# First two token tiles in large rows over both hardware queues ahead of the weights, half-chunk first weights; last store contiguous, last sum seeded in PSUM

## The chip, the cores and the metric

The kernel runs on all 8 cores of one Trainium2 chip, each core on its own share of the batch with the same weights and no exchange between the cores. The metric is the device time of the slowest core, in microseconds (us).

A run on all eight cores has two states. In the fast state every core shows a mean granted TensorE clock of 0.998 to 1.000. In the slow state the cores of one die, or of both, show less (a mean of 0.81 to 0.99), and the run is 1% to 21% longer. In the slow profile of the kernel before, on its slowest core, the clock is 0.81 in some stretches and 1.00 in others (0.81 from 260 to 270 us, 1.00 from 280 to 360), with TensorE busy in both. Only fast runs, or the cores of an undisturbed die in a slow run, are compared below.

## The reference, cut to what matters

```python
def rmsnorm(x, g):
    y = x * rsqrt(mean(x * x, axis=-1, keepdims=True) + EPS)
    return y * g

def swiglu(h, w_gate, w_up, w_down):
    return (silu(h @ w_gate) * (h @ w_up)) @ w_down

for i in range(4):                                   # layers
    x = x + 0.5 * rmsnorm(swiglu(rmsnorm(x, g[0]), ...first FFN...), g[1])
    x = x +       rmsnorm(mixer(rmsnorm(x, g[2])), g[3])   # gated convolution or causal pooling
    x = x + 0.5 * rmsnorm(swiglu(rmsnorm(x, g[4]), ...second FFN...), g[5])
```

The width is 1,024 features (8 chunks of 128) and the FFN is 2,816 wide (22 chunks). Each core does two passes over 1,056 tokens, held as three tiles of 352 tokens, with the features on the 128 partitions.

## The kernel before

The program is a list of operations that a small scheduler in Python puts into a fixed order on each engine, before anything runs. It knows the engines' durations, and it has a model of DMA: one serial pipe.

```python
# Sched.run(): when the result of an operation is assumed to be visible
            vis = o.end
            if o.dma:
                s0 = max(dma_free, st + (2.8 if e == "pool" else 1.0))
                dma_free = s0 + o.dma[1] / 170e3
                vis = dma_free + 1.5
```

The start of the program, which the change rewrites. Queues: `sp` and `act` are hardware queues, `pool` is the GpSimd queue, which carries all weights in this program; they are converted from f32 to bf16 on the way (the page of the kernel before counts 636.49 MB read from HBM and 339.98 MB in DMA packets):

```python
    # earlier in the program: params on the sp queue, 128 rows of 1 KB
    LEAD = 2

    def first_group(finish, pre):
        load_x(0, 0, ("sp", "act", "sp", "act"), 4, -3)        # tile 0 in quarters, 2,816 B rows
        slots = [load_ab(0, 0, jj) for jj in range(LEAD)]      # weight chunks 0 and 1 (1 MB each)
        load_x(0, 1, "pool", 2)                                # tile 1 behind them
        slots += [load_ab(0, 0, jj) for jj in range(LEAD, GRP)]
        load_wdn(0, 0)
        load_x(0, 2, "pool", 2)
        warm(72, ["ones"])                                     # warm-up matmuls with ones
        prenorm(0, 0, 0, pre=False, parts=(2, 2, 2, 1, 1))     # statistics of tile 0 in five groups
        prenorm(0, 0, 1, pre=False)
        prenorm(0, 0, 2)
        for k in range(GRP + LEAD):
            if k < GRP:
                ffn_ab(0, 0, k, slots[k], k == 0)              # tile 0 leads by two chunks
            if k >= LEAD:
                ffn_ab(1, 1, k - LEAD, slots[k - LEAD])
        # ... cut: down projections, tile 2
```

The statistics of a tile are eight squares on ScalarE, summed over the features by matmuls with a matrix of ones:

```python
    def norm_stats(t, src, key, off, parts=(8,)):
        v = S.vt(stat=True)
        for c in range(NCH):
            S.op("act", lambda a, c=c: a.activation(out=h[t][:, c, :], in_=src[:, c, off:off + TS], func=AF.Square), ...)
        # ... cut: matmuls with ones in groups of `parts`, then Ln and Exp on ScalarE give rr = 1/rms
```

The end: the last tile's down projection in halves of 176 tokens. For each chunk, VectorE adds the PSUM sum to the accumulator, ScalarE squares it; then Ln, Exp, two wide multiplications and additions, and the store:

```python
        for dc, hc in pairs:
            def fo(pe, v=v, dc=dc, c0=c0):
                for jj in range(GRP):
                    mm = pe.matmul(B(v)[:, 0:HW], lhsT=wdn[dc][...], rhs=gt[u][:, jj, c0:c0 + HW],
                                   start=(jj == 0), stop=(jj == GRP - 1))
                return mm
            S.op("dve", ... out=acc, in0=B(v)[:, 0:HW], in1=acc, op=ALU.add ...)
            S.op("act", ... out=sq, in_=acc, func=AF.Square ...)
            # ... cut
            for q in range(2):
                # ... cut: acc *= rr; x += acc, four chunks at a time
                S.op("sp", lambda e, o=o, c0=c0: e.dma_start(
                    out=y_o[p, t].rearrange("p (a b) -> p a b", b=TS)[:, o:o + 4, c0:c0 + HW],   # 704 B rows
                    in_=x[t][:, o:o + 4, c0:c0 + HW]), ...)
```

## Time and profile before

| | us |
|---|---|
| fast runs | 4354.1, 4354.21 |
| slow runs | 4509.77, 5136.39 |
| span of the profiled run (slow, clock 0.974 on its slowest core) | 4453.2 |

The profile of the kernel before fell in the slow state, so its 4,453 us is not a time to compare with. The head and the tail can still be read from it, with that in mind.

From the page of the kernel before: the first line of part 1 (busy us, share of the span, instructions), the ScalarE queue's line of part 3 (packets, MB, share of the DMA engines) and two groups of part 5 (busy us, mean ns of one, idle time before them and what ended it).

```profile
PE 4430.3 (99%) x29109; PEld 2878.7 (65%) x29109; DVE 2187.6 (49%) x3807; ACT 1743.8 (39%) x3053; POOL 460.6 (10%) x973
...
q10 hardware_dynamic: 288, 0.72, 0.1%
...
L357 PE MATMUL ps<-h,ring 128*128 128x352 bf16 x19200 | 2981.6, 318 | 4.9 <-DVE h L357 4.9
...
L357 PE MATMUL ps<-gt,wdn 128*128 128x352 bf16 (+1 forms) x9304 | 1423.8, 315 | 0.6 <-DVE gt L357 0.6
```

TensorE is busy 99% of the span. Nothing that leaves the 28,504 weight matmuls alone can move the time by more than what lies before the first and after the last of them, and the few us of gaps in between. All instructions carry one line number, because one helper emits them; so they are told apart by their tiles: `ring` holds gate and up weights, `wdn` down weights, `x` the tokens, `h` the squares and then the normalised tokens, `rr` 1/rms.

The head, from the timeline of the kernel before on its slowest core (start us, duration us, engine, operation, out<-in, count, idle time before it and what ended it):

```profile
7.17 1.65 ACT L357 ACTIVATE h<-x 128x352 bf16<-128x352 f32 x4 [3.59 <-DMA x<-x_in]
...
11.73 1.65 ACT L357 ACTIVATE h<-x 128x352 bf16<-128x352 f32 x4 [2.91 <-DMA x<-x_in]
...
13.44 1.35 PE L357 MATMUL ps<-h,ones_bf 128*128 128x352 bf16 x4 [3.24 <-ACT h L357]
...
15.39 0.46 ACT L357 ACTIVATE rr<-ps 128x352 f32<-128x352 f32 x1
...
15.89 4.05 DVE L357 SCALAR_TENSOR_TENSOR h<-x,params_sb,rr 128x352 bf16<-128x352 f32 x8
...
16.62 7.73 PE L357 MATMUL ps<-h,ring 128*128 128x352 bf16 x32 [1.83 <-DVE h L357]
...
26.80 1.37 PE L357 MATMUL ps<-h,ones_bf 128*128 128x352 bf16 x8 [2.44 <-ACT h L357]
...
28.00 4.19 PE L357 MATMUL ps<-h,ring 128*128 128x352 bf16 x27
```

The same stretch in the fast profile of this kernel (first experiment), on its slowest core; the count of the last row ends where the query's window ended:

```profile
15.30 0.46 ACT L357 ACTIVATE rr<-ps 128x352 f32<-128x352 f32 x1
...
16.52 6.73 PE L357 MATMUL ps<-h,ring 128*128 128x352 bf16 x32 [1.83 <-DVE h L357]
...
26.90 5.27 PE L357 MATMUL ps<-h,ring 128*128 128x352 bf16 x23
```

Four squares run on an early half of tile 0 at 7.17 and the other four when its second half is there, at 11.73. Statistics, Ln, Exp and the first normalised chunk follow, and the first weight matmul starts at 16.62. TensorE pauses once more at 26.8, for the statistics of tile 1, and from 28.0 it doesn't stop.

The tail, from the chain of waits of the kernel before (start us, duration us, what):

```profile
4429.96 12.47 PE ps L357 x162
...
4444.64 0.26 DVE acc L357
4444.90 0.02 issue
4444.93 0.36 ACT sqf L357
...
4446.40 1.69 DVE acc L357 x2
4448.09 0.80 DVE x L357
```

After the last weight matmul come a sum on VectorE, a square, Ln and Exp, wide VectorE work and the store: some 8.8 us on this core, in which TensorE has only the last statistics to do.

### The profile page before, as it was taken

The numbers are of one execution on the slowest core, as the hardware profiler recorded it, in microseconds if no ns is written. First come the engines' busy times: TensorE is split into PE (matmuls) and PEld (weight loads), VectorE is DVE, ScalarE is ACT, GpSimd is POOL, SyncE is SP. The second block draws the span as 40 slices with busy tenths as digits, with TensorE's granted clock in tenths as the row PEclk, the third lists the DMA queues.
The fourth block names the chain that finished last, engine by engine and source line by source line (L and its number), as shares of the span: only waits on it lengthen the run. The fifth ranks groups of instructions, "written<-read, shape, count | busy, mean of one in ns | idle before, by whom it ended". The sixth has DMA issues, their size and how long they took to land.

```text
span 4453.2 us, 68545 instructions; the slowest of 8 cores (4392.4 to 4453.2 us)
## 1 busy us (share of the span) xinstructions
PE 4430.3 (99%) x29109; PEld 2878.7 (65%) x29109; DVE 2187.6 (49%) x3807; ACT 1743.8 (39%) x3053; POOL 460.6 (10%) x973
## 2 busy tenths in 40 slices
PE   9999999999999999999999999999999999999999
PEld 5666666666666666666666666666666666666666
DVE  2376261755347525175434753527452474352844
ACT  3244242643334424264333442326433344232643
POOL 1021000000002100000000210000000021000000
PEclk9999999999999999999999999999999999999999
DMA  7445444434344544443544354444443334444441
GB/s 134 68 76 90 79 79 79 79 53 73 60 68 70 86 79 79 79 79 67 107 93 71 62 86 79 79 79 79 70 77 60 65 58 80 79 79 79 79 77 43
DMA packets 106673, 339.98 MB, mean 76 GB/s; under 512 B 11904, under 2 KB 15360, under 8 KB 106368
## 3 DMA queue, kind: packets, MB, share of 16 engines
q0 software_dynamic: 98352, 315.40, 43.4%
q1 hardware_dynamic: 7728, 19.48, 1.3%
q8 instruction: 229, 3.75, 0.4%
q10 hardware_dynamic: 288, 0.72, 0.1%
q14 instruction: 76, 0.62, 0.1%
HBM read 636.49 MB, written 11.55 MB: 146 GB/s over the span
## 4 chain that ended last, share of the span: by engine, by line
PE 99%; DVE 0%; DMA 0%; ACT 0%; issue 0%; DVEq 0%; ACTq 0%
PE ps L357 99%; DMA x<-x_in 0%; ACT h L357 0%; DVE acc L357 0%; DVE h L357 0%; DVE x L357 0%; ACT ps L357 0%; ACT rr L357 0%; DVEq L375 0%; DVE gt L357 0%; ACT sa L357 0%; ACT acc L357 0%; ACTq L357 0%; ACT sqf L357 0%
## 5 line engine op out<-in xcount | busy, mean ns | idle before, releaser
L357 PE MATMUL ps<-h,ring 128*128 128x352 bf16 x19200 | 2981.6, 318 | 4.9 <-DVE h L357 4.9
L357 PEld LDWEIGHTS ps<-h,ring 128*128 128x128 bf16 x19200 | 1905.3, 99 | 1042.9 <-DVE h L357 4.7
L357 PE MATMUL ps<-gt,wdn 128*128 128x352 bf16 (+1 forms) x9304 | 1423.8, 315 | 0.6 <-DVE gt L357 0.6
L357 DVE TENSOR_TENSOR gt<-ps,sa 128x352 bf16<-128x352 f32 x1056 | 551.5, 523 | 1668.6 <-PE ps L357 1623.6
L357 PEld LDWEIGHTS ps<-gt,wdn 128*128 128x128 bf16 x9304 | 914.7, 99 | 484.6 <-DVE gt L357 1.0
L357 ACT ACTIVATE sa<-ps 128x352 f32<-128x352 f32 x1152 | 533.8, 464 | 1516.5 <-PE ps L357 1484.4
L357 POOL DMA_DIRECT2D ring<-wab x352 | 186.8, 532 | 2681.4 <-PE ps L357 2672.1
L357 ACT ACTIVATE acc<-ps 128x352 f32<-128x352 f32 x480 | 222.5, 465 | 466.0 <-PE ps L357 466.0
L357 DVE TENSOR_TENSOR h<-h 128x704 f32<-128x704 f32 (+1 forms) x404 | 320.4, 793 | 69.0 <-ACT h L357 66.5
L357 ACT ACTIVATE h<-acc 128x352 bf16<-128x352 f32 (+2 forms) x181 | 145.9, 814 | 473.3 <-DVE acc L357 450.2
L357 DVE TENSOR_TENSOR acc<-ps,acc 128x352 f32<-128x352 f32 (+1 forms) x392 | 202.5, 517 | 255.4 <-PE ps L357 254.4
L357 ACT ACT_TABLE_LOAD x239 | 306.6, 1283 | 7.6 <-PEq L400 2.0
L357 DVE SCALAR_TENSOR_TENSOR h<-x,params_sb,rr 128x352 bf16<-128x352 f32 x480 | 246.7, 578 | 117.6 <-ACT rr L357 117.4
L357 ACT ACTIVATE h<-x 128x704 f32<-128x704 f32 (+2 forms) x266 | 216.0, 832 | 56.6 <-DVE x L357 29.8
L357 DVE TENSOR_TENSOR x<-x,acc 128x1408 f32<-128x1408 f32 (+1 forms) x146 | 232.9, 1596 | 0.2
L357 DVE SCALAR_TENSOR_TENSOR acc<-acc,params_h,rr 128x352 f32<-128x352 f32 x376 | 198.0, 578 | 43.0 <-ACT rr L357 42.9
L357 POOL DMA_DIRECT2D wdn<-wd x256 | 135.6, 534 | 327.8 <-PE ps L357 327.5
L357 DVE SCALAR_TENSOR_TENSOR scr<-scr,params_sb 128x352 f32<-128x352 f32 (+1 forms) x192 | 112.1, 584 | 9.2 <-ACT scr L357 8.7
L357 ACT ACTIVATE scr<-scr,params_sb 128x352 f32<-128x352 f32 (+1 forms) x96 | 56.7, 591 | 95.5 <-DVE scr L357 95.5
L357 ACT ACTIVATE ps<-ps,epst 128x352 f32<-128x352 f32 (+1 forms) x145 | 76.2, 526 | 35.3 <-PE ps L357 31.5
L357 DVE TENSOR_TENSOR scr<-ps,sa 128x352 f32<-128x352 f32 (+2 forms) x128 | 54.8, 428 | 36.1 <-PE ps L357 34.1
L357 POOL COPY scr<-convh 128x2 f32<-128x2 f32 x96 | 42.3, 446 | 266.3 <-DVE pinit L357 177.2
(58 smaller groups left out, 889.4 us busy)
## 6 DMA issues: line engine op xcount, KB each, us to landing
ring<-wab POOLq DMA_DIRECT2D x352, 512.0 KB, 10.9
wdn<-wd POOLq DMA_DIRECT2D x256, 352.0 KB, 14.9
ring<-wci POOLq DMA_DIRECT2D x29, 768.0 KB, 12.1
wdn<-wco POOLq DMA_DIRECT2D x32, 256.0 KB, 11.6
y_o<-x SPq DMA_DIRECT2D x10, 704.0 KB, 3.2
x<-x_in SPq DMA_DIRECT2D x6, 704.0 KB, 6.9
x<-x_in POOLq DMA_DIRECT2D x4, 704.0 KB, 37.0
scr<-spool SPq DMA_DIRECT2D x4, 608.0 KB, 10.8
```

The costliest lines, as they stand in the source:

```text
L357: ins = attr(*a, **k)
```

## The change: its intent and its diff

The intent is a shorter head and a shorter tail. In the head, tiles 0 and 1 go in halves, in rows of 5,632 B, to both hardware queues, ahead of the weights in the program; the first weight chunk comes in two halves, so that TensorE can begin with half of it; four of the eight squares go to VectorE; more warm-up matmuls; and the lead of two chunks is dropped, because both tiles are expected together. In the tail, the last sum is seeded in PSUM by a ScalarE copy, so that the matmuls add to it, and the stores are contiguous and the last is split over two queues.

```diff
+    def norm_stats(t, src, key, off, parts=(8,), dsq=0):
         for c in range(NCH):
+            if c >= NCH - dsq:
+                S.op("dve", lambda v_, c=c: v_.tensor_tensor(out=h[t][:, c, :], in0=src[...], in1=src[...], op=ALU.mult), ...)
+                continue
             S.op("act", ... func=AF.Square ...)
 ... (cut)
     def first_group(finish, pre):
-        load_x(0, 0, ("sp", "act", "sp", "act"), 4, -3)
-        slots = [load_ab(0, 0, jj) for jj in range(LEAD)]
-        load_x(0, 1, "pool", 2)
-        slots += [load_ab(0, 0, jj) for jj in range(LEAD, GRP)]
+        load_x(0, 0, ("sp", "act"), 2, -3)
+        S.op("sp", lambda e: e.dma_start(out=params[:], in_=params_d), 0.06, writes=["params"], dma="params", nbytes=70000, prio=-3)
+        small_params()
+        load_x(0, 1, ("sp", "act"), 2, -3)
+        slots = [[load_units(wab[0, 0][:, i * 1024:(i + 1) * 1024], 1)[0] for i in range(2)]]
+        slots += [load_ab(0, 0, jj) for jj in range(1, GRP)]
         load_wdn(0, 0)
         load_x(0, 2, "pool", 2)
-        warm(72, ["ones"])
-        prenorm(0, 0, 0, pre=False, parts=(2, 2, 2, 1, 1))
-        prenorm(0, 0, 1, pre=False)
+        warm(115, ["ones"])
+        prenorm(0, 0, 0, pre=False, parts=(4, 2, 2), dsq=4)
+        prenorm(0, 0, 1, pre=False, parts=(4, 2, 2), dsq=4)
         prenorm(0, 0, 2)
-        for k in range(GRP + LEAD):
-            if k < GRP:
-                ffn_ab(0, 0, k, slots[k], k == 0)
-            if k >= LEAD:
-                ffn_ab(1, 1, k - LEAD, slots[k - LEAD])
+        for k in range(GRP):
+            ffn_ab(0, 0, k, slots[k], k == 0)
+            ffn_ab(1, 1, k, slots[k], k == 0)
 ... (cut: the convolution history waits for the first weights; tail:)
+            seed = (hc, dc) == (1, NCH - 1)
+            if seed:
+                S.op("act", lambda a, ...: a.activation(out=B(v)[:, 0:HW], in_=acc[t][:, dc, a0:a0 + HW], func=AF.Copy), ...)
-                                   start=(jj == 0), stop=(jj == GRP - 1))
+                                   start=(jj == 0 and not seed), stop=(jj == GRP - 1), skip_group_check=seed)
 ... (cut: with seed, no VectorE sum, and the squares read PSUM)
-                S.op("sp", ... out=y_o[p, t].rearrange("p (a b) -> p a b", b=TS)[:, o:o + 4, c0:c0 + HW] ...)
+                S.op("act" if (hc, d) == (1, 4) else "sp", ...
+                        out=y_o[p, t][:, (hc * NCH + d) * HW:(hc * NCH + d + n) * HW] ...)    # 2,816 or 1,408 B rows
```

That the matmuls add to what ScalarE has written is shown here by results alone: every experiment below with the seed (e2 to e7, e9 to e12) is marked correct in the record. By the program's order an earlier matmul has written the bank; a seed in a bank that none had written was not run.

More of the change, by code (lines that the diff above doesn't have):

```diff
@@ L467, in build_program @@
     P_STAT, P_EV, P_CH = -2, 0, 1
-    S.op("sp", lambda e: e.dma_start(out=params[:], in_=params_d), 0.06, writes=["params"], dma="params", nbytes=90000)
     S.op("dve", lambda v: v.memset(ones_bf[:], 1.0), 0.2, writes=["ones"])
@@ L478, in build_program @@
             S.op("pool", lambda v, g=g, i=i: v.memset(invc[:, g, i:i + 1], 1.0 / (i + 1)), 0.2, writes=[("invc", g)], prio=-2)
-    S.op("dve", lambda v: v.tensor_scalar(out=params_h[:], in0=params[:, 0:192], scalar1=0.5, scalar2=None, op0=ALU.mult),
-         0.3, reads=["params"], writes=["params_h"])
-    S.op("dve", lambda v: v.tensor_copy(out=pscale[:].rearrange("p a b -> p (a b)"), in_=params[:, 240:256]), 0.2,
-         reads=["params"], writes=["pscale"])
-    S.op("dve", lambda v: v.tensor_scalar(out=pscale[:, :, 0:2], in0=pscale[:, :, 0:2], scalar1=0.5, scalar2=None, op0=ALU.mult),
-         0.2, reads=["pscale"], writes=["pscale"])
-    for j in range(2):
-        gp = ((2 * j + 1) * 6 + 3) * 8
-        S.op("dve", lambda v, j=j, gp=gp: v.tensor_tensor(out=pgain[:, j], in0=pscale[:, j], in1=params[:, gp:gp + 8], op=ALU.mult),
-             0.2, reads=["pscale", "params"], writes=[("pgain", j)])
     st = {"ru": 0, "ld": 0, "q": 0, "u": 0, "z": 0, "w": 0}
@@ L521, in stat_finish @@
              2 * c_act(TS) + 0.15, reads=["eps"], writes=[("rr", b)], vts=[v], prio=P_CH, margin=0.2, tbl="lnexp", wvt=True)
-    def norm_stats(t, src, key, off, parts=(8,)):
+    def norm_stats(t, src, key, off, parts=(8,), dsq=0):
         v = S.vt(stat=True)
         for c in range(NCH):
+            if c >= NCH - dsq:
+                S.op("dve", lambda v_, c=c: v_.tensor_tensor(out=h[t][:, c, :], in0=src[:, c, off:off + TS], in1=src[:, c, off:off + TS], op=ALU.mult),
+                     c_dve(TS), reads=[(key, t, c)], writes=[("h", t, c)], prio=P_CH, margin=0.1)
+                continue
             S.op("act", lambda a, c=c: a.activation(out=h[t][:, c, :], in_=src[:, c, off:off + TS], func=AF.Square),
@@ L585, in norm_stats_out, with prenorm @@
         stat_finish(t, v)
-    def prenorm(l, n, t, to_u=False, pre=True, parts=(8,), ag=False):
+    def prenorm(l, n, t, to_u=False, pre=True, parts=(8,), ag=False, dsq=0):
         b = t % 2
@@ L591, in prenorm @@
         else:
-            norm_stats(t, x[t], "x", 0, parts)
+            norm_stats(t, x[t], "x", 0, parts, dsq)
         if ag:
@@ L718, in ffn_out_last, with fo @@
             c0, a0 = hc * HW, PAD + hc * HW
-            def fo(pe, v=v, dc=dc, c0=c0):
+            seed = (hc, dc) == (1, NCH - 1)
+            if seed:
+                S.op("act", lambda a, v=v, dc=dc, a0=a0: a.activation(out=B(v)[:, 0:HW], in_=acc[t][:, dc, a0:a0 + HW], func=AF.Copy),
+                     c_act(HW), reads=[("acc", t, dc), ("out", dc - 3)], vts=[v], prio=P_EV)
+            def fo(pe, v=v, dc=dc, c0=c0, seed=seed):
                 for jj in range(GRP):
                     mm = pe.matmul(B(v)[:, 0:HW], lhsT=wdn[dc][:, jj * 128:(jj + 1) * 128], rhs=gt[u][:, jj, c0:c0 + HW],
-                                   start=(jj == 0), stop=(jj == GRP - 1))
+                                   start=(jj == 0 and not seed), stop=(jj == GRP - 1), skip_group_check=seed)
@@ L724, in fo @@
                 return mm
-            S.op("pe", fo, GRP * 0.081, reads=[("g", u, jj) for jj in range(GRP)] + [("wdn", dc)], vts=[v])
+            S.op("pe", fo, GRP * 0.081, reads=[("g", u, jj) for jj in range(GRP)] + [("wdn", dc)], writes=[("out", dc)], vts=[v])
             ak = ("accl", hc, dc)
-            S.op("dve", lambda v_, v=v, dc=dc, a0=a0: v_.tensor_tensor(
-                out=acc[t][:, dc, a0:a0 + HW], in0=B(v)[:, 0:HW], in1=acc[t][:, dc, a0:a0 + HW], op=ALU.add),
-                c_dve(HW), reads=[("acc", t, dc)], writes=[ak], vts=[v], prio=P_EV)
@@ L730, in ffn_out_last @@
-            S.op("act", lambda a, dc=dc, a0=a0, hc=hc: a.activation(out=sq[hc][:, dc, 0:HW], in_=acc[t][:, dc, a0:a0 + HW], func=AF.Square),
-                 c_act(HW, True), reads=[ak], writes=[("sq", hc, dc)], prio=P_EV)
+            if not seed:
+                S.op("dve", lambda v_, v=v, dc=dc, a0=a0: v_.tensor_tensor(
+                    out=acc[t][:, dc, a0:a0 + HW], in0=B(v)[:, 0:HW], in1=acc[t][:, dc, a0:a0 + HW], op=ALU.add),
+                    c_dve(HW), reads=[("acc", t, dc)], writes=[ak], vts=[v], prio=P_EV)
@@ L732, in ffn_out_last @@
+            y = lambda v=v, dc=dc, a0=a0, seed=seed: B(v)[:, 0:HW] if seed else acc[t][:, dc, a0:a0 + HW]
+            S.op("act", lambda a, dc=dc, hc=hc, y=y: a.activation(out=sq[hc][:, dc, 0:HW], in_=y(), func=AF.Square),
+                 c_act(HW, True), reads=[] if seed else [ak], writes=[("sq", hc, dc)], vts=[v] if seed else [], prio=P_EV)
             g = gcol(l, 5, dc)
-            S.op("act", lambda a, dc=dc, a0=a0, g=g: a.activation(out=acc[t][:, dc, a0:a0 + HW], in_=acc[t][:, dc, a0:a0 + HW], func=AF.Copy,
-                                                                 scale=params_h[:, g:g + 1]),
-                 c_act(HW, True) + 0.09, reads=[ak, "params_h"], writes=[ak], prio=P_CH)
+            S.op("act", lambda a, dc=dc, a0=a0, g=g, y=y: a.activation(out=acc[t][:, dc, a0:a0 + HW], in_=y(), func=AF.Copy,
+                                                                      scale=params_h[:, g:g + 1]),
+                 c_act(HW, True) + 0.09, reads=["params_h"] + ([] if seed else [ak]), writes=[ak], vts=[v] if seed else [], prio=P_CH)
@@ L754, in ffn_out_last @@
             bc = bass.AP(rv.tensor, rv.offset, [list(rv.ap[0]), [0, 4], [1, HW]])
-            for q in range(2):
-                o = 4 * q
+            tb_ = (t + 2 * hc) % NTILE
+            yb = hq[tb_].rearrange("p a b -> p (a b)").rearrange("p (a b) -> p a b", b=HW)
+            yk = [("h", tb_, c) for c in range(NCH)]
+            for o in (0, 4):
                 ks = [("accl", hc, o + i) for i in range(4)]
@@ L760, in ffn_out_last @@
                     c_dve(4 * HW), reads=ks + [("rr", hc)], writes=ks, prio=P_CH)
-                S.op("dve", lambda v_, o=o, a0=a0, c0=c0: v_.tensor_tensor(
-                    out=x[t][:, o:o + 4, c0:c0 + HW], in0=x[t][:, o:o + 4, c0:c0 + HW], in1=acc[t][:, o:o + 4, a0:a0 + HW], op=ALU.add),
-                    c_dve(4 * HW), reads=ks + xk, writes=[("xl", hc, q)], prio=P_CH)
-                S.op("sp", lambda e, o=o, c0=c0: e.dma_start(
-                    out=y_o[p, t].rearrange("p (a b) -> p a b", b=TS)[:, o:o + 4, c0:c0 + HW], in_=x[t][:, o:o + 4, c0:c0 + HW]), 0.06,
-                    reads=[("xl", hc, q)], dma=f"yl{hc}{q}", nbytes=4 * HW * 256, final=True)
+                for d, n in ((o, 4),) if hc == 0 or o == 0 else ((o, 2), (o + 2, 2)):
+                    S.op("dve", lambda v_, d=d, n=n, a0=a0, c0=c0, yb=yb: v_.tensor_tensor(
+                        out=yb[:, d:d + n, :], in0=x[t][:, d:d + n, c0:c0 + HW], in1=acc[t][:, d:d + n, a0:a0 + HW], op=ALU.add),
+                        c_dve(n * HW), reads=ks + xk, writes=[("yl", hc, d)] + yk, prio=P_CH)
+                    S.op("act" if (hc, d) == (1, 4) else "sp", lambda e, d=d, n=n, hc=hc, yb=yb: e.dma_start(
+                        out=y_o[p, t][:, (hc * NCH + d) * HW:(hc * NCH + d + n) * HW],
+                        in_=yb[:, d:d + n, :].rearrange("p a b -> p (a b)")), 0.06,
+                        reads=[("yl", hc, d)], dma=f"yl{hc}{d}", nbytes=n * HW * 256, final=True)
     def load_ab(f, g, jj):
@@ L787, in ffn_group, with small_params @@
                 ffn_out(g, t, u, finish, pre(t))
-    LEAD = 2
-    def first_group(finish, pre):
-        load_x(0, 0, ("sp", "act", "sp", "act"), 4, -3)
-        slots = [load_ab(0, 0, jj) for jj in range(LEAD)]
-        load_x(0, 1, "pool", 2)
-        slots += [load_ab(0, 0, jj) for jj in range(LEAD, GRP)]
+    def small_params():
+        S.op("dve", lambda v: v.tensor_scalar(out=params_h[:], in0=params[:, 0:192], scalar1=0.5, scalar2=None, op0=ALU.mult),
+             0.3, reads=["params"], writes=["params_h"])
+        S.op("dve", lambda v: v.tensor_copy(out=pscale[:].rearrange("p a b -> p (a b)"), in_=params[:, 240:256]), 0.2,
+             reads=["params"], writes=["pscale"])
+        S.op("dve", lambda v: v.tensor_scalar(out=pscale[:, :, 0:2], in0=pscale[:, :, 0:2], scalar1=0.5, scalar2=None, op0=ALU.mult),
+             0.2, reads=["pscale"], writes=["pscale"])
+        for j in range(2):
+            gp = ((2 * j + 1) * 6 + 3) * 8
+            S.op("dve", lambda v, j=j, gp=gp: v.tensor_tensor(out=pgain[:, j], in0=pscale[:, j], in1=params[:, gp:gp + 8], op=ALU.mult),
+                 0.2, reads=["pscale", "params"], writes=[("pgain", j)])
+    def first_group(finish, pre):
+        load_x(0, 0, ("sp", "act"), 2, -3)
[4 more added lines that the diff above has]
+        slots += [load_ab(0, 0, jj) for jj in range(1, GRP)]
         load_wdn(0, 0)
         load_x(0, 2, "pool", 2)
-        warm(72, ["ones"])
-        prenorm(0, 0, 0, pre=False, parts=(2, 2, 2, 1, 1))
-        prenorm(0, 0, 1, pre=False)
+        warm(115, ["ones"])
+        prenorm(0, 0, 0, pre=False, parts=(4, 2, 2), dsq=4)
+        prenorm(0, 0, 1, pre=False, parts=(4, 2, 2), dsq=4)
         prenorm(0, 0, 2)
-        for k in range(GRP + LEAD):
-            if k < GRP:
-                ffn_ab(0, 0, k, slots[k], k == 0)
-            if k >= LEAD:
-                ffn_ab(1, 1, k - LEAD, slots[k - LEAD])
+        for k in range(GRP):
+            ffn_ab(0, 0, k, slots[k], k == 0)
+            ffn_ab(1, 1, k, slots[k], k == 0)
         ffn_out(0, 0, 0, finish, True)
@@ L914, in conv_mixer @@
         S.op("sp", lambda e: e.dma_start(out=chist[:].rearrange("p a b -> p (a b)"), in_=sconv[j, p]), 0.06,
-             writes=["chist"], dma="chist", nbytes=65536)
+             reads=[("ru", 0)], writes=["chist"], dma="chist", nbytes=65536)
         slots = [load_units(wci[j, c], 3) for c in range(NCH)]
@@ L1035, in load_x @@
                                                  in_=x_in[p, t][:, n * i * TS:(i + 1) * n * TS]), 0.55 if eng == "pool" else 0.1,
-                 writes=[("x", t, c) for c in range(n * i, n * i + n)], dma=f"x{eng}{t}{i}", nbytes=n * TS * 350, prio=-1 if eng == "pool" else prio)
+                 writes=[("x", t, c) for c in range(n * i, n * i + n)], dma=f"x{eng}{t}{i}", nbytes=n * TS * (350 if eng == "pool" else 271), prio=-1 if eng == "pool" else prio)
     def store_y(p, t):
@@ L1151, in unpack @@
         pss = np.asarray(r["ps_s"]).reshape(2, NPASS, 128, NCH, NSS, 19)[..., 4:19].transpose(0, 1, 4, 5, 3, 2)
+        yl = np.asarray(r["y_o"])[-1, -1].reshape(128, 2, NCH, TS // 2)
+        y[-1, NTOK - TS:] = yl.transpose(1, 3, 2, 0).reshape(TS, D)
         for p in range(NPASS):
```

## The prediction

> **What bounds the kernel now.** The page has TensorE 99% busy and the chain of waits 99% TensorE: 28,504 weight matmuls (19,200 + 9,304) of 315 to 318 ns. The change touches none of them, only the two ends, which are small (slowest core, 4):
>
> - Head (timeline). Token tile 0 lands at 11.7 us; its first weight matmul starts at 16.6; 32 of them (4.8 us at full rate) are done before 28.0, when TensorE stops pausing. So the head loses 28.0 - 4.8 = 23.2 us: 22 to 23 on cores 1, 3, 4, 7, about 20 on 0, 2, 5, 6, whose tile 0 landed at 9.2 to 9.9 us.
> - The DMA engines are over 90% busy from 4 us on (stretch table)[...]: a contest for bytes.
> - The granted clock is 0.50 in 15-20 us; four statistics matmuls took 1.35 us against 0.77 warm.[...]
> - Tail (chain of waits): last weight matmul to end of span about 8.8 us, of it DVE sum 0.34, square 0.36, Ln and Exp 0.7, wide DVE work 3.3, and over 3 us of store.
>
> **What the change does.**
> 1. Tiles 0 and 1 in 5,632 B rows on both hardware queues; tile 1 no longer behind 2 MB of weights. [...]the DMA table shows one packet per row (288 for two 128-row loads and completions)[...]. Estimate, from 0.72 MB in 4.0 to 4.5 us now: tile 0 at about 10 us (-1.5), tile 1 at 15 to 18 instead of 20 to 22. But all eight squares now follow the landing (about 2.1 us, DVE and ACT sharing, against 1.66), and weights get less.
> 2. [...]last statistics about 0.5 us against 1.37. Landing to first weight matmul: 4.9 to about 4.5.
> 3. The lead of two chunks goes. Each chunk feeds 4.8 us of TensorE[...], but tile 1's normalisation (0.5 us a chunk on DVE against 0.15 a matmul) is now exposed, where tile 0's next chunk covered it. This gives back part: head -2 us (+1 to -5) on the slow cores.
> 4. Tail: the seed in PSUM saves the last DVE sum, -0.4; rows of 1,408 to 2,816 B instead of 704 and a half-sized last store, -0.6.
>
> The body is unchanged but for ripples of list scheduling; its gaps (3.2, 1.1, 1.1 us) stay.
>
> **Predicted:** 4354.2 - 3 = **4351 us**, 80% range **4341 to 4362**[...]. Chances: faster by over 2% 0.01, within 2% 0.97, slower by over 2% 0.02 (only if the slow state takes the median; one of three runs before was 5136).
>
> **What would show it.** Tile 0's squares start near 10 us on cores 1, 3, 4, 7; clock 1.0 when weight matmuls start; head loss about 21 us; last weight matmul to end near 7.8; body equal.
>
> **What would make it wrong.** Tile 1 landing at 20 us, so that TensorE stands before it and the head grows; or at 13, and the head shrinks by 6; first weights starved; a changed body order.

The sum is -2 for the head and -1 for the tail (-0.4 and -0.6), together the -3 in 4354.2 - 3 = 4351. The gain of the tokens from larger rows (tile 0 at about 10 us, tile 1 at 15 to 18) and the last statistics in about 0.5 us stand as estimates. (Of the 288 packets, the packet records of the kernel before have 256 rows of 2,816 B and 32 of 4 B.)

## The result, and the profile after

| | fast runs, us | their mean | slow runs, us |
|---|---|---|---|
| before | 4354.1, 4354.21 | 4354.16 | 4509.77, 5136.39 |
| after | 4354.05, 4354.2, 4355.34, 4356.14 | 4354.93 | 5003.51 |

The median of the four runs of after that the result counts is 4355.17 us; 4355.34 is a fifth run. A ratio here is the mean time of one kernel's fast runs over that of the other's in the same rounds, so it is not quite the ratio of those medians. It is 1.0002, with a 95% interval of 0.9978 to 1.0026: +0.8 us between the means (+0.6 without the fifth run), and nothing that these runs can tell from zero. Forecast were -3 us.

Three stretches add up to each core's span: the start to the first down-projection matmul ("head", a fixed amount of work lies in it), from there to the end of the last weight matmul ("body"), and the rest ("tail"). The fast profile of the kernel before comes from the first experiment.

| | before, median of 8 cores (range) | after | difference of medians |
|---|---|---|---|
| first weight matmul starts | 14.8 (13.6 to 16.5) | 19.9 (17.9 to 20.8) | +5.0 |
| head | 74.1 (72.7 to 76.3) | 76.2 (74.0 to 77.4) | +2.0 |
| body | 4266.9 (4266.9 to 4267.3) | 4267.2 (4265.9 to 4268.1) | +0.4 |
| tail | 8.55 (8.52 to 8.61) | 7.70 (7.65 to 8.00) | -0.85 |
| span | 4349.7 (4348.1 to 4351.7) | 4351.5 (4347.5 to 4352.5) | +1.7 |

The slowest cores, which set the time, differ by less than the medians, 4351.7 against 4352.5. And a median of eight cores is itself uncertain: in the kernel before, four cores start their weight matmuls at 13.6 to 13.9 us and four at 15.8 to 16.5, so that 14.8 is no core's; its two profiles (one slow, one fast) differ by 0.6 us in median head and lost time. Differences of that size between kernels are not read as effects below.

A second measure of the head is used below, "lost": 130 us less 0.1495 us for each weight matmul whose weights were loaded by then. It counts waiting, stretches at a lower clock and statistics together. It is 21.3 us before and 23.3 us after (medians; largest core 23.6 and 24.6).

The same lines of the page of the kernel after:

```profile
PE 4332.1 (100%) x29152; PEld 2846.5 (65%) x29152; DVE 2189.0 (50%) x3815; ACT 1736.9 (40%) x3044; POOL 459.7 (11%) x972
...
q10 hardware_dynamic: 432, 1.62, 0.1%
...
L357 PE MATMUL ps<-h,ring 128*128 128x352 bf16 x19200 | 2905.7, 313 | 6.3 <-DVE h L357 6.3
...
L357 PE MATMUL ps<-gt,wdn 128*128 128x352 bf16 (+1 forms) x9304 | 1399.5, 311 | 2.5 <-DMA wdn<-wd 1.8
```

The number of weight matmuls is the same. The ScalarE queue (q10) carries 1.62 MB instead of 0.72: the halves of tiles 0 and 1, and half of the last store (0.18 MB). This profile is fast (313 ns a matmul), so its idle column may be compared with the fast profile of before, and two things are new in it: 4.1 of the 6.3 us that wait for `h` are one wait in the head, and 1.8 us wait for down weights, once, at 2,219 us, in the middle of the program.

The head, from the timeline of the kernel after on its slowest core:

```profile
9.87 1.65 ACT L357 ACTIVATE h<-x 128x352 bf16<-128x352 f32 x4 [6.28 <-DMA x<-x_in]
...
11.00 1.83 DVE L357 TENSOR_TENSOR h<-x 128x352 bf16<-128x352 f32 x4 [7.12 <-DMA x<-x_in]
...
11.58 2.09 PE L357 MATMUL ps<-h,ones_bf 128*128 128x352 bf16 x8 [2.95 <-ACT h L357]
...
14.26 0.46 ACT L357 ACTIVATE rr<-ps 128x352 f32<-128x352 f32 x1
...
16.90 0.53 DVE L357 TENSOR_TENSOR h<-x 128x352 bf16<-128x352 f32 x1 [4.07 <-DMA x<-x_in]
...
19.12 4.05 DVE L357 SCALAR_TENSOR_TENSOR h<-x,params_sb,rr 128x352 bf16<-128x352 f32 x8
...
19.84 2.17 PE L357 MATMUL ps<-h,ring 128*128 128x352 bf16 x5 [4.08 <-DVE h L357]
...
21.80 2.55 PE L357 MATMUL ps<-h,ones_bf 128*128 128x352 bf16 x8
...
24.15 8.10 PE L357 MATMUL ps<-h,ring 128*128 128x352 bf16 x48
```

Tile 0's statistics are ready at 14.72 (14.26 + 0.46), against 15.76 on the slowest core in the fast profile of the kernel before. But the normalised tokens are made on VectorE, and there the scheduler has put the four squares of tile 1 first. VectorE waits 4.07 us for tile 1's data, does the squares with the small parameter operations between them, and only at 19.12 begins the normalisation that TensorE stands waiting for. Then five weight matmuls run, and the statistics of tile 1 at a clock of 0.50 (2.55 us for eight). From 24.15 TensorE runs through, 2.8 us earlier than in the fast profile of before (26.90 on its slowest core), but it has done 5 weight matmuls by then instead of 32.

The granted clock in these stretches, from the stretch table of the kernel after (stretch and its length, then busy us and count of PE, PEld, DVE, ACT and POOL, granted clock, DMA share, GB/s):

```profile
15.00:20.00 5.00, 0.92 (x10) 0.69 (x7) 3.10 (x11) 0.29 (x1) 1.13 (x5) 0.84 1.08 267
20.00:25.00 5.00, 4.96 (x16) 2.15 (x16) 3.17 (x7) 1.93 (x6) 0.00 (x0) 0.50 1.03 161
```

The clock is 0.50 from 20 to 25 us, where the weight matmuls begin, after 4.08 us with nothing for TensorE. The extra warm-up matmuls ran before that wait: the last 21 of all 115 started at 13.46 and took 2.31 us, and the clock was 1.00 from 10 to 12 us and 0.50 from 13 to 15. What they do for the clock these runs don't show.

The tail, from the chain of waits of the kernel after:

```profile
4330.35 14.44 PE ps L357 x188
4344.79 0.02 issue
4344.81 0.32 ACT sqf L357
...
4346.41 1.69 DVE acc L357 x2
4348.10 0.81 DVE h L357
...
4348.94 0.54 DVE h L357
...
4349.50 0.52 DVE h L357
```

The square follows the last matmul directly: 0.04 us from the end of the last weight matmul to the square, against 0.54 in the fast profile of before. From the end of the last VectorE operation to the end of the span it is 2.5 us against 3.2. Splitting the last addition costs 0.3 us of that back. The tail does what it was made for.

When the loads landed, from the packet records of the two fast profiles (end of the last packet, us, range over all eight cores):

| load | before | after |
|---|---|---|
| tile 0, last packet | 8.8 to 10.9 | 8.0 to 9.4 |
| first weight chunk | 12.4 to 13.4 | halves at 14.4 to 15.2 and 18.2 to 19.6 |
| tile 1 | 20.5 to 22.3 | halves at 14.1 to 17.1 and 17.6 to 20.0 |
| second weight chunk | 16.2 to 18.1 | 19.9 to 21.8 |

Tile 1 did come earlier, by about 2.5 us; the first weight chunk came 6 us later. On core 2 of the kernel after, tile 0's last packet ended at 9.03 us and the squares on it began only at 11.00, 1.97 us later. The first weight load was issued at 2.5 us; on the 16 cores of the first profiles of before and after its first packet began at 6.5 to 8.5 us, so 4 to 6 us after the issue. No run here tells why.

### The profile page after: what moved, and what is told of

It is laid out like the page before. It is cut to its first block, busy times and chain, and to the rows that moved or that the text cites. A ratio compares the mean times of both kernels' runs of the same rounds, so it can differ in the third digit from the quotient of the medians.

```text
span 4352.5 us, 68638 instructions; the slowest of 8 cores (4347.5 to 4352.5 us)
## 1 busy us (share of the span) xinstructions
PE 4332.1 (100%) x29152; PEld 2846.5 (65%) x29152; DVE 2189.0 (50%) x3815; ACT 1736.9 (40%) x3044; POOL 459.7 (11%) x972
## 3 DMA queue, kind: packets, MB, share of 16 engines
q10 hardware_dynamic: 432, 1.62, 0.1%
## 4 chain that ended last, share of the span: by engine, by line
PE 98%; DMA 1%; DVE 0%; ACT 0%; issue 0%; ACTq 0%
PE ps L357 98%; DMA wdn<-wd 1%; DMA x<-x_in 0%; DVE h L357 0%; DVE acc L357 0%; ACT acc L357 0%; DVE gt L357 0%; ACTq L357 0%; ACT rr L357 0%; ACT sqf L357 0%; ACT ps L357 0%; DVE params_h L357 0%; DVE pscale L357 0%; DVE pgain L357 0%
## 5 line engine op out<-in xcount | busy, mean ns | idle before, releaser
L357 PE MATMUL ps<-h,ring 128*128 128x352 bf16 x19200 | 2905.7, 313 | 6.3 <-DVE h L357 6.3
L357 PEld LDWEIGHTS ps<-h,ring 128*128 128x128 bf16 x19200 | 1878.7, 98 | 994.2 <-issue 4.2
L357 PE MATMUL ps<-gt,wdn 128*128 128x352 bf16 (+1 forms) x9304 | 1399.5, 311 | 2.5 <-DMA wdn<-wd 1.8
L357 DVE TENSOR_TENSOR x<-x,acc 128x1408 f32<-128x1408 f32 x142 | 229.4, 1616 | 0.2
L357 ACT ACTIVATE ps<-ps,epst 128x352 f32<-128x352 f32 (+1 forms) x145 | 76.2, 526 | 35.1 <-PE ps L357 34.0
L357 ACT ACTIVATE rr<-ps 128x352 f32<-128x352 f32 (+1 forms) x145 | 67.0, 462 | 4.6
## 6 DMA issues: line engine op xcount, KB each, us to landing
wdn<-wco POOLq DMA_DIRECT2D x32, 256.0 KB, 15.8
scr<-spool SPq DMA_DIRECT2D x4, 608.0 KB, 12.4
```

The lines of the kernel that those rows point to most:

```text
L357: ins = attr(*a, **k)
```

## The experiments

Two theories for the lost head stood at the start. Theory A, order: the scheduler's model has tile 1 landing at about 12 us, so VectorE is made to wait for it; with the true landing times in the model the gain would appear. Theory B, bytes: whatever the order, tile 1 and the parameters now take transfer time that the first weights need, so TensorE would wait for weights instead. "Turns" in the expectations of e6 to e8 is the estimate that queues which are at work together move equal numbers of rows, so that larger rows get more bytes; the counts that fit it, from two profiles, stand under "bytes or order" below (22, 17 and 20 rows in one us). The runs were made in four sessions on three chips; times are compared with those of the kernel before in the same rounds.

### e1_before_again

No edit: the kernel before.

> The kernel before, unchanged, run as if it were an experiment: it gives the size of the noise and a profile of before in the fast state, which is missing so far. Ratio 1.0000 within 0.0005. In the profile the first down-projection matmul should start near 74.7 us (median of the cores; 72.8 to 76.1 in the profile of before) and the tail (last weight matmul to end of span) near 8.55 us. If the first figure came out near 76 in the fast state, the head of the changed kernel (76.15) would have lost nothing and my reading would fall.

Measured: fast runs 4353.02 to 4354.13 us (five) against 4352.89 to 4353.95 of the same kernel in the same rounds, ratio 1.0 (0.9986 to 1.0014). Lost 21.3 us, tail 8.55 us. This is the scale: the same kernel differs by about 1 us from run to run (by up to 2.6 us in the rounds of e7).

### e2_tail_only

Edit: the kernel before with the whole tail part of the change (seed, contiguous stores, split last store), and nothing of the head.

```diff
 # on the kernel before
+            seed = (hc, dc) == (1, NCH - 1)
 ... (the tail part of the change as shown above, nothing else)
```

> Before plus the tail part alone (seed in PSUM, contiguous stores, split last store). Theory: the tail's share works as predicted and the head of the change gives it back; so here the tail is 7.7 us instead of 8.55, first down-projection matmul as in before, time about 0.9 us shorter (ratio 0.9998). Rival: the tail's gain never reaches the measured time; then the tail in the profile is shorter but the spans stay.

Measured: fast runs 4352.94, 4353.05 and 4353.64 us, five slow ones, ratio 0.9999 (0.9983 to 1.0015). The profile fell in the slow state; on its undisturbed die the tail is 7.72 us and the lost time of the head is as before (20.1 to 23.6 us). The tail's gain of 0.85 us is real in the trace and stays whatever the head does. In the times it is hidden by the 1 us between runs.

### e3_order

Edit: the kernel after with nothing but the landing times that the scheduler assumes moved to those measured.

```diff
-                vis = dma_free + 1.5
+                vis = dma_free + 1.5 + o.late
 ... (cut)
-        load_x(0, 0, ("sp", "act"), 2, -3)
+        load_x(0, 0, ("sp", "act"), 2, -3, 4.5)
 ... params +7.0, tile 1 +9.0, weight chunks +2.6
```

> The changed kernel with the same instructions; only the landing times that its list scheduler assumes for the first loads are moved to those of the trace (tile 0 near 11 us, params near 14, tile 1 near 20, weights 2.6 us later), so the order on the engines changes. Theory A (wrong order: VectorE is sent to tile 1's squares before tile 0's normalisation and stands 4 us for tile 1's load): the first weight matmul moves from 19.9 us (median) to 14.5 to 17.5, when params have landed, and the first down-projection matmul from 76.15 to about 73.5; time 2 to 3 us below the changed kernel. Rival B (bytes: the first weights and tile 1 land too late whatever the order): the first weight matmul moves but the first down-projection matmul stays within 1 us of 76.

Measured: fast runs 4354.37 to 4357.35 us (four), ratio 1.0004 (0.999 to 1.0019). Lost 24.2 us (after: 23.3). The timeline of this kernel, core 7:

```profile
15.38 0.26 DVE L358 TENSOR_SCALAR params_h<-params_sb 128x192 f32<-128x192 f32 x1 [3.01 <-DMA params_sb<-params]
...
15.63 0.58 DVE L358 SCALAR_TENSOR_TENSOR h<-x,params_sb,rr 128x352 bf16<-128x352 f32 x1
...
17.57 0.48 PE L358 MATMUL ps<-h,ring 128*128 128x352 bf16 x1 [4.68 <-DMA ring<-wab]
...
19.82 4.62 PE L358 MATMUL ps<-h,ring 128*128 128x352 bf16 x15 [1.77 <-DMA ring<-wab]
```

VectorE no longer waits for tile 1 before tile 0, and the first normalised chunk is there at 16.2. It was of no use: VectorE stands idle for 3.01 us until the parameters are there, and TensorE until the first weights are (4.68 us of idle time, which overlaps VectorE's; 1.4 of it come after the first normalised chunk), and then 1.77 us for their second half. The first weight matmul does start at 17.3 us (median) instead of 19.9, as theory A had it, but the first down-projection matmul comes at 77.1, 1 us later than in the kernel after. The order alone is not the cause, so theory A falls as the whole explanation, and B is supported. (With the late landing assumed, the scheduler also puts 32 matmuls of tile 0 ahead of tile 1's statistics again, so this run has the old lead back too, and it doesn't help either.)

### e4_tile1_squares_act

Edit: the kernel after with tile 1's squares all on ScalarE again, to take the wait out of VectorE's queue.

```diff
-        prenorm(0, 0, 1, pre=False, parts=(4, 2, 2), dsq=4)
+        prenorm(0, 0, 1, pre=False, parts=(4, 2, 2))
```

> The changed kernel with all eight squares of tile 1 on ScalarE, nothing else; TensorE's order stays as in the changed kernel. Theory A: tile 0's normalisation is no longer held up, so the first weight matmul starts near 14.5 to 17.5 us (params), but TensorE's own order has tile 1's statistics after five weight matmuls, so the first down-projection matmul gains nothing and may lose 1 to 2 us (76 to 78): one held-up queue is swapped for another. Rival B expects no move of either beyond 1 us.

Measured: one look, 4354.2 us; first weight matmul at 19.9, lost 23.4. The expectation was missed, and the run does not separate the theories. The timeline of core 2 shows why:

```profile
16.73 1.65 ACT L357 ACTIVATE h<-x 128x352 bf16<-128x352 f32 x4 [4.81 <-DMA x<-x_in]
...
18.29 0.51 ACT L357 ACTIVATE ps<-ps,epst 128x352 f32<-128x352 f32 x1
...
19.32 4.05 DVE L357 SCALAR_TENSOR_TENSOR h<-x,params_sb,rr 128x352 bf16<-128x352 f32 x8 [2.33 <-ACT rr L357]
```

The wait for tile 1 moved to ScalarE, where the squares of tile 1 now stand before the Ln of tile 0. The same assumed landing, another engine.

### e5_params_front

Edit: the kernel after with the parameters in two halves ahead of tile 0, one on each hardware queue.

```diff
+        for e_, o_, k_ in (("sp", 0, "params"), ("act", 64, "params2")):
+            S.op(e_, lambda e, o_=o_: e.dma_start(out=params[o_:o_ + 64, :], in_=params_d[o_:o_ + 64, :]), 0.06, writes=[k_],
+                 dma=k_, nbytes=35000, prio=-4)
         load_x(0, 0, ("sp", "act"), 2, -3)
-        S.op("sp", lambda e: e.dma_start(out=params[:], in_=params_d), 0.06, writes=["params"], dma="params", nbytes=70000, prio=-3)
```

> The changed kernel, but the parameter load (128 rows of 1 KB) goes first, split over both hardware queues, instead of standing on one queue between tile 0 and tile 1. Theory[...]: tile 1's late half lands near 16.5 us instead of 19, level with the other half, first weight matmul 2 to 3 us earlier than 19.9, TensorE time lost by 130 us about 21 instead of 23.3. Rival (the bytes alone set the landings[...]): tile 1's late half stays within 1 us of 19 and the lost time within 0.7 us.

Measured: only slow times (4589.11 and above); the undisturbed die 1 of the profile has lost 24.5 to 26.1 us and its first weight matmul at 21.5 to 22.0. The parameters had landed by 4.1 us. But tile 0's second half came late, as the timeline of core 4 shows (8.95 for the first half's squares, 13.80 for the second's):

```profile
8.95 1.65 ACT L359 ACTIVATE h<-x 128x352 bf16<-128x352 f32 x4 [4.32 <-DMA x<-x_in]
...
13.80 1.84 DVE L359 TENSOR_TENSOR h<-x 128x352 bf16<-128x352 f32 x4 [8.10 <-DMA x<-x_in]
```

The ScalarE queue moved its first packet of the tile only at 4.2 to 6.6 us (6.6 on core 4), the other hardware queue at about 3. Why is left open. Tile 1's late half landed at 18.3 to 19.6, as in the kernel after: freeing the queue of the parameters did not bring it forward, which fits a contest for bytes.

### e6_first_chunk_whole

Edit: the kernel after with the first weight chunk as one load (rows of 8 KB read, 4 KB written) instead of two halves.

```diff
-        slots = [[load_units(wab[0, 0][:, i * 1024:(i + 1) * 1024], 1)[0] for i in range(2)]]
-        slots += [load_ab(0, 0, jj) for jj in range(1, GRP)]
+        slots = [load_ab(0, 0, jj) for jj in range(GRP)]
```

> The changed kernel, but the first weight chunk is loaded whole (8 KB rows read) instead of in two halves (4 KB rows). Theory of turns: the whole first chunk lands near 15 to 16 us, where its second half landed at 19 (median); tile 1 is at most 1 us later. Because the order of the changed kernel makes the first weight matmul wait for tile 1 anyway, the lost time stays within 1 us of 23.3. Rival (bytes): the first chunk is complete at 18 to 19 in either form.

Measured: only slow times; die 0 of the profile is undisturbed (spans 4350.7 to 4357.2 us). The chunk was complete at 15.3 us (14.8 to 16.3) instead of 19, and tile 1's late half at 21 instead of 19. With rows of twice the size the weights' queue got more bytes in the same time, and tile 1 got fewer: in this run what one queue gained, the others lost. Lost rose to 24.3 to 27.1 us, against an expectation within 1 us of 23.3: on core 2 TensorE waits 5.4 us before the first weight matmul and 3.0 us right after it, both behind squares of tile 1, because the order is still that of an early tile 1.

### e7_three_mended

Edit: the kernel after with all three mended: parameters first, whole first chunk, and assumed landing times near those measured.

```diff
 ... (the edits of e5 and e6, and)
-        load_x(0, 1, ("sp", "act"), 2, -3)
+        load_x(0, 1, ("sp", "act"), 2, -3, 6.5)
 ... tile 0 +2.5, weight chunks +1.0, tile 2 +5.0
```

> The changed kernel with all three: parameters first, first weight chunk whole, and the scheduler told later landings (so tile 0 is normalised before tile 1 is squared). If order and turns together are what ate the head's gain: first weight matmul near 14.5 us, first chunk near 14 to 15, tile 1 near 16.5 to 17.5, TensorE time lost by 130 us 18.5 to 20 (changed kernel 23.3, before 21.3), tail 7.7; time about 3 us below before (ratio 0.9993) and below the changed kernel. If bytes alone set it, lost time stays above 21.5 and the time is that of before.

Measured: fast runs 4351.56, 4352.06 and 4352.34 us against 4352.56 to 4355.18 before (six) in the same rounds, ratio 0.9996 (0.9974 to 1.0017). (A seventh run of before, 4379.44 us, counts as fast, but two of its cores show a clock of 0.992; the ratio leaves it out.) Lost 22.4 us: better than after, still 1 us worse than before, and short of the 18.5 to 20 expected. That the times are nevertheless no worse than before comes from the slowest core: its head is as long (76.2 us, before 76.3), and the tail is shorter. The first weight matmul starts at 19.1. Tile 0's second half again came late, as in e5 (its squares at 15.7 us on core 3). Three repairs of the changed head don't bring back the old one.

### e8_big_rows_before

Edit: the kernel before with tile 0 alone in two halves of 5,632 B rows.

```diff
-        load_x(0, 0, ("sp", "act", "sp", "act"), 4, -3)
+        load_x(0, 0, ("sp", "act"), 2, -3)
```

> Before, with tile 0 alone loaded in two halves of 5.6 KB rows instead of four quarters of 2.8 KB rows; nothing else. Theory of turns: tile 0 lands 0.7 to 1.5 us earlier (median of the last packet from about 10 to 9 us), the first weight chunk 0.7 to 1.5 us later than 12.7. Squares start after the whole tile, so the first weight matmul gains at most 0.5 us (15.0 median before). Rival (bytes): tile 0 lands within 0.4 us of before and the first chunk too.

Measured: one fast run, 4353.79 us. A second run was slow (4974.81). The last packet of tile 0 landed at 9.3 us (median) instead of 9.75, the first weight chunk at 12.7 instead of 13.1. So the large rows gain about half a microsecond for tile 0, less than the turn argument promised (0.7 to 1.5), and the weights behind them did not come later, as it also had: the run is nearer to the other of the two expectations. But the first weight matmul starts at 17.0 instead of 14.8, and lost is 23.3 instead of 21.3. On core 2 all eight squares run as one row of 3.20 us from 8.79, and the statistics only from 11.27:

```profile
8.79 3.20 ACT L357 ACTIVATE h<-x 128x352 bf16<-128x352 f32 x8 [5.70 <-DMA x<-x_in]
...
15.81 7.23 PE L357 MATMUL ps<-h,ring 128*128 128x352 bf16 x32 [1.83 <-DVE h L357]
```

With quarters, half of the squares are done while the other half is still landing. With halves that land together, that overlap is gone, and it was worth 2 us when ScalarE does all squares. (The kernel after shares them with VectorE and so pays less of it.)

### e9_tile1_behind_weights

Edit: the kernel after with tile 1 back on the weights' queue behind the first two chunks. Everything else of the change stays: halves of tile 0, shared squares, half-chunk first weights, warm-up, no lead, tail.

```diff
         small_params()
-        load_x(0, 1, ("sp", "act"), 2, -3)
         slots = [[load_units(wab[0, 0][:, i * 1024:(i + 1) * 1024], 1)[0] for i in range(2)]]
-        slots += [load_ab(0, 0, jj) for jj in range(1, GRP)]
+        slots += [load_ab(0, 0, 1)]
+        load_x(0, 1, "pool", 2)
+        slots += [load_ab(0, 0, jj) for jj in range(2, GRP)]
```

> The changed kernel with tile 1's load put back on the weights' queue behind the first two chunks; large rows of tile 0, halved first chunk, shared squares, tail and the loop order without the lead stay. If bringing tile 1 forward is what ate the head's gain (it pushes the first chunks back by what it gains, and the order on VectorE waits for it): first weight matmul near 14.5 to 15.5 us (19.9 in the changed kernel), second half of the first chunk near 14 instead of 19, TensorE time lost by 130 us 20 to 21.5 (23.3 in the changed kernel, 21.3 before). If instead the large rows or the halved chunk ate it, the lost time stays above 22.5.

Measured: one look, 4351.86 us, all cores fast (spans 4346.4 to 4350.0 us, after 4347.5 to 4352.5). Lost 20.7 us against 23.3 after and 21.3 before; first weight matmul at 14.8. The halves of the first chunk landed at 10.4 to 12.6 and 13.2 to 15.7 instead of about 15 and 19. The timeline of core 2, to be read against the kernel after on the same core:

```profile
13.28 0.46 ACT L357 ACTIVATE rr<-ps 128x352 f32<-128x352 f32 x1
...
14.08 4.05 DVE L357 SCALAR_TENSOR_TENSOR h<-x,params_sb,rr 128x352 bf16<-128x352 f32 x8
...
14.80 5.53 PE L357 MATMUL ps<-h,ring 128*128 128x352 bf16 x32 [0.95 <-DVE h L357]
...
22.95 2.46 PE L357 MATMUL ps<-h,ones_bf 128*128 128x352 bf16 x8 [2.61 <-ACT h L357]
```

From Exp to the normalisation is 0.3 us instead of 4.4, and 32 weight matmuls run without a wait for weights of more than 0.3 us. One load put back moves the head by 2.6 us: tile 1 ahead of the weights accounts for the 2 us that the head lost. Of the gain that had been forecast (-2) only 0.6 us against before is left, no more than the two profiles of before differ. This edit changes the bytes, and with them the order: tile 1 is assumed later, so the scheduler again runs 32 weight matmuls of tile 0 ahead of tile 1's statistics. It therefore shows the cause to be the move of tile 1 with all that follows from it, and not bytes or order each by itself. The dropped lead was not tested alone either; e3 has the lead and the order back, with tile 1 still ahead of the weights, and the head stayed lost.

### e10_tile1_after_one_chunk and e11_before_order_shared_squares

Two candidates built up from the kernel before: shared squares and the tail, once with a lead of one chunk (tile 1 behind one weight chunk), once with the order of before.

```diff
 # both, on the kernel before: dsq and the tail as in the change
 # e10: LEAD = 1
 # both:
-        warm(72, ["ones"])
-        prenorm(0, 0, 0, pre=False, parts=(2, 2, 2, 1, 1))
-        prenorm(0, 0, 1, pre=False)
+        warm(96, ["ones"])
+        prenorm(0, 0, 0, pre=False, parts=(2, 2, 2, 2), dsq=2)
+        prenorm(0, 0, 1, pre=False, parts=(4, 2, 2), dsq=4)
```

> Before with the tail of the change, tile 0 in quarters as before but its last two squares on VectorE, more warm-up, and tile 1 behind one weight chunk instead of two (its last four squares on VectorE). If the head is set by the bytes that must land before tile 1 can run: tile 1 lands near 18 instead of 21.5 us, second chunk near 21, TensorE time lost by 130 us about 19.5 to 20.5 (21.3 before), tail 7.7, time about 2 us below before (ratio 0.9995). If it is not, lost time stays at 21 to 22 and only the tail's 0.9 us is gained.

Measured: two fast runs, 4351.81 and 4352.79 us, four slow ones, no ratio. Lost 20.1 us, within the 19.5 to 20.5 expected and the least of all kernels; the body is 4268.1 us, 1.3 more than before, so little of it arrives.

> As the last, with tile 1 behind two chunks as before: only the tail, the shared squares and the longer warm-up of the change. First weight matmul 0.5 to 1 us earlier than 14.8 (median) but the head still waits for tile 1: lost time 20.5 to 21.3, time about 1 us below before (ratio 0.9998).

Measured: fast runs 4350.52, 4352.03 and 4352.08 us against 4352.61 to 4353.9 before, ratio 0.9996 (0.9976 to 1.0016). Lost 20.6 us, body 4267.6 (+0.7). The head's median is 0.7 us shorter than before, no more than the two profiles of before differ, and the edit has more warm-up matmuls beside the shared squares; the first weight matmul starts at 15.4 (median), later than the 13.8 to 14.3 expected.

### e12_tile1_behind_weights_timed

Edit: none against e9; the same kernel in timed rounds.

> The kernel of the ninth run again, now timed in rounds, as the version that should beat both kernels: TensorE time lost by 130 us near 20.7, tail 7.7, so its fast runs 1 to 2 us below those of before (ratio 0.9996, before about 4353.4) and 2 to 3 below the changed kernel. If its single time of 4351.86 was luck, the ratio is 0.9999 or above.

Measured: fast runs 4351.19, 4351.22, 4351.62 and 4351.79 us against 4352.76 to 4354.15 us of before (eight) in the same rounds, ratio 0.9995 (0.998 to 1.0011). Lost 21.0 us, first down-projection matmul at 73.9, tail 7.75 us. The two sets of fast runs don't overlap, and the gain is about 2 us against before, near the -3 that had been forecast for the whole change. But it does not come where the forecast had it: by medians of the cores the tail gives 0.8 us, the body 0.5 and the head 0.2 to 0.3. And it is 0.05%, and the interval of the ratio contains 1. Of the kernels with several fast runs it has the lowest ratio; e7 and e11 (0.9996 each) cannot be told from it. By the ratios it is 3 us (0.07%) below the kernel after, with which it was not run side by side.

## Why the prediction was right or wrong

**What bounds the kernel: right.** TensorE is 99 to 100% busy in both profiles with the same matmuls, and no kernel that has a ratio is more than 0.05% from the kernel before.

**The size and place of the tail (item 4): right.** Forecast -1.0 in two parts (-0.4 and -0.6); measured 8.55 to 7.70 us, -0.85, in the changed kernel and in e2 alone. The seed gave 0.5 us between the last matmul and the square, of which 0.1 went back between square and Exp; the store gave 0.8, of which 0.3 went back to the third addition.

**The head (items 1 to 3): wrong, and this is the step that failed.** The prediction said "head -2 us (+1 to -5) on the slow cores". Measured: +2.0 us of lost time and +2.0 us to the first down-projection matmul, as medians of the eight cores; on the four cores with the longest heads +1.2 us, and on the core that sets the span +0.4. Term by term:

- "tile 0 at about 10 us (-1.5)": the squares of its second half start at 11.00 on core 2, against 11.63 on the slowest core of before, run again (-0.6); e8 measured the rows alone at 0.45 us. In e8 the first weight chunk came 0.4 us earlier too; there was little to win.
- "tile 1 at 15 to 18 instead of 20 to 22": its two halves came at 14 to 17 and 18 to 20. The late half, which counts, is some 2 us later than forecast.
- "weights get less" was named and given no size. It was the large term: the first chunk complete at about 19 instead of 13 us. Moving tile 1 back (e9) put it at 13.2 to 15.7.
- "Landing to first weight matmul: 4.9 to about 4.5": it became 8.8 us on core 2 (11.00 to 19.84). The prediction followed the chain of data from tile 0 to TensorE, and did not ask in which order each engine would take up its work. VectorE had tile 1's squares before tile 0's normalisation and waited 4.07 us for their data. (Of the 4.4 us between Exp and the normalisation, about 1.4 would have gone to the parameters in any case: they were there at 16.1.)
- "last statistics about 0.5 us against 1.37": from the last square of tile 0 to Ln it is 0.87 us on core 2 (12.83 to 13.70) against 1.46 on the slowest core of before, where about 0.5 had been forecast. In the wait that followed TensorE had nothing for 4.08 us, the clock stood at 0.50 after it, and the statistics of tile 1 took 2.55 us.

The prediction's own list of what would make it wrong had "Tile 1 landing at 20 us, so that TensorE stands before it and the head grows". That is nearly the case that came, except that VectorE stood before tile 1 and TensorE behind VectorE.

**Which of the two is the cause, bytes or order?** Both limits lie at nearly the same place, which fits that each repair alone failed. Mending the order (e3) left waits for the parameters and for both halves of the first weights. Mending one load (e6) made another one late by 2 us. Taking tile 1's bytes away (e9) removed both, and changed the order with them. The packet records of the kernel after on core 2 between 10 and 13 us show how it was shared: the three queues end 22, 17 and 20 packets in one us, 17, 22 and 19 in the next, 18, 16 and 19 in the third, though one carries 1 KB rows, one 5.6 KB and one 2 KB (4 KB read). The counts are nearly equal, whatever the size of the rows; what makes them so the records don't show. With two other queues at work the weights had one row in three here. In the fast profile of before, on core 1 in the same 3 us, one other queue is at work and again the counts are equal (31, 35 and 33 rows of the weights, 31, 34 and 32 of the other), and a weight row there is 4 KB written: about 33 rows of 4 KB a us became 19 of 2 KB. The prediction counted the larger rows as a gain of the tokens and gave the weights' loss no size.

**"The body is unchanged but for ripples of list scheduling": roughly right, but the ripple is as large as what was forecast for the whole change.** On all cores of the kernel after, about 1 us of waiting for `h` near the turn to the second pass has gone (sum 3.0 to 2.2 us); on five of eight cores a wait of 1.2 to 1.8 us for a down-projection load has come at 2,219 us. On core 2, which set the span, the body is 1.2 us longer than on the slowest core before: 76.7 + 4268.1 + 7.7 = 4352.5 us, against 76.3 + 4266.9 + 8.55 = 4351.7 us on the slowest core before. The wait comes and goes with small changes of the first group (none on six cores of e9, up to 1.7 us in e12 with the same kernel). What sets it was not tried and is open.

**The sum.** Forecast -2 - 1 = -3; measured by medians of the cores +2.0 + 0.4 - 0.85 = +1.6, and on the slowest core +0.4 + 1.2 - 0.85 = +0.8, which the measured +0.8 us between the means fits, though a difference so small is within the noise. The sign of the head was wrong. That the time stayed in the stated range says nothing for the prediction: the range is 21 us wide, seven times the forecast change.

## What to carry to other kernels

The loads of this head shared DMA engines that were busy throughout (a share of 0.98 to 1.08 in each stretch from 5 to 30 us, on core 2 of the kernel after), and the load that was moved forward took its bytes from what it passed: the first weight chunk came 6 us later. So write down what lands later, with a number, before counting what lands earlier. With engine queues in a fixed order, ask of each early load not only who needs it but what stands behind its first user in that engine's queue: here 4 us of VectorE's waiting for tile 1 held up tile 0, which was there. And in a kernel that is 99% matmul, the ripple of the rest of the schedule (1 to 2 us here) is as large as the last gains at the ends, so read head, body and tail apart before believing a total.
